# Moving tiles read alternately from their two halves, and products of 512 columns in place of 256 and 256

## The chip, the cores and the metric

The kernel runs on one core of a Trainium2 chip. Time is device time in microseconds; before the change the median of three runs is 1071.56 us (1071.44 to 1072.94). The engines meant below are TensorE (PE, with its weight loads, PEld), VectorE (DVE), ScalarE (ACT), GpSimd (POOL) and the DMA queues.

## What is computed

One layer of a hybrid decoder on 512 tokens of 1024 features, in float32: a gated feed-forward block, a mixer of two branches (spatial gating and a state-space scan), a second feed-forward block, gated embeddings and a last norm.

```python
def swiglu(x, w_gate, w_up, w_down):
    return (jax.nn.silu(x @ w_gate) * (x @ w_up)) @ w_down

h = h + 0.5 * swiglu(rmsnorm(h, ffn1_norm[i]), ffn1_w_gate[i], ffn1_w_up[i], ffn1_w_down[i])
proj = rmsnorm(h, mix_norm[i]) @ w_in[i]
u, v, z, xbc, dt_raw = jnp.split(proj, IN_SPLITS, axis=-1)
...
h = h + jnp.concatenate([ya, yb], axis=-1) @ w_out[i]
h = h + 0.5 * swiglu(rmsnorm(h, ffn2_norm[i]), ffn2_w_gate[i], ffn2_w_up[i], ffn2_w_down[i])
gate = jax.nn.sigmoid(rmsnorm(h, ple_norm[i]) @ ple_w_gate[i] + ple_b_gate[i])
h = h + gate * (p[i] @ ple_w_proj[i])
```

The feed-forward width is 2816, the input projection has 4624 columns (spatial gating 2 x 1024, z 1024, the convolved part 1536, 16 time steps).

## The kernel before

**Layout.** Features lie on the 128 partitions, tokens along the free dimension: the state `h` is eight tiles of 128 x 512. A matmul multiplies a stationary 128x128 piece of weights with a moving tile of tokens (up to 512 columns, one bank of PSUM) and adds into the bank. The moving tile is what the matmul streams column by column. Only the product for v is the other way round: there a chunk of 128 tokens is stationary and the weights move.

**Precision.** Every float32 operand of a large product is split into a rounded part hi and a rest lo (type float32r), and a product is three matmuls: hi x hi, hi x lo, lo x hi. The split of weights is `cast` on ScalarE (L532) and `low` on VectorE (L536), each 128x1024.

**Products, and the lines that issue them.**

- L746 (`Group.product`): gate and up products of ten of the eleven groups of the feed-forward block, done by a scheme of seven products of half size in place of eight. Each works on 256 tokens, so that a bank holds two results of 256 columns. Its inputs `xfa` and `xfb` (`XForms`, `Early`) hold pieces of 256 columns, hi beside lo.
- L835 (`plain_steps`): the first group of each block, without that scheme, for both halves of the tokens. The first input tile of a bank takes two matmuls over 512 columns and two over 256; the others take six over 256.
- L248 (`accumulate`): the down products (called with `halves`, eight output tiles, 22 input tiles), the output projection (all 512 columns, 16 input tiles) and the gates of the embedding (five with `halves`, three done one half after the other at the end of the kernel, `gate_half`).
- L232 (`passes`): the input projections, 28 units of 512 columns, and v, in widths of 272, 256 and 512.
- L1055 (`embedding`): the product of the per-layer embedding, two halves each.
- L338 (`spread`): a matmul with ones, which gives the norm's factor of each token to all partitions; its result is kept in a tile `r`, with which gate, up and projection results are multiplied.

**What reads the banks.** L951 adds a down product to `h`; `convin`, `z` and `u` are made from projections and `r` (L1225, L1478, L1621); L1679 adds the output projection; L1742 starts the gates at the end. L893 to L904 make the product of gate and up, `g`, and L915 and L917 split it into `ghi` and `glo`, the moving tiles of the down products.

**Order.** The work is a list of steps (`Step`: load, split, product, what comes after). `run` issues them in a fixed order, a hand-written string `ENTRY` moves pieces of them, and the order on TensorE, ScalarE, VectorE and the SP queue is the order of the program. Weights come in blocks of 512 KB over the SP queue, some with an adding DMA over the GpSimd queue. Of the eight banks three are called `mm`, two `a`, three `sm`.

Of the kernel before, what the change touches and what calls it, by code (L numbers as in the profile page):

```python
# [31 lines left out]
P = 128  # L32
# [80 lines left out]
def layer_kernel(ctx: ExitStack, tc: tile.TileContext, a: dict, out: bass.AP):  # L113
# [105 lines left out]
    def scaled_split(h, name, k):  # L219
# [18 lines left out]
    def accumulate(ps, w, j0, xs, first=True, last=True, parts=whole):  # L238

        whi, wlo = w  # L240
        for k, (xhi, xlo) in enumerate(xs):
            c = slice((j0 + k) * P, (j0 + k + 1) * P)
            by_part = [(n, tok) for tok in parts for n in range(3)]
            if k == 0 and parts is halves:
                by_part = [(0, whole[0]), (1, whole[0]), (2, halves[0]), (2, halves[1])]
            for i, (n, tok) in enumerate(by_part):
                wt, xt = ((whi, xhi), (whi, xlo), (wlo, xhi))[n]
                nc.tensor.matmul(  # L248
                    ps[:, tok], wt[:, c], xt[:, tok], start=first and k == i == 0,
                    stop=last and k == len(xs) - 1 and i == len(by_part) - 1, skip_group_check=True,  # L250
                )
# [22 lines left out]
    class Norm:  # L274
# [59 lines left out]
        @staticmethod  # L334
        def spread(diags, ps=None):
# [16 lines left out]
        def behind(self, steps, n, use):  # L352


            got = {}

            def sums():
                got["ps"] = self.sums()

            def spread():  # L360
                diags = self.diagonals(self.of_sums(got["ps"], n))
                got["ps"] = self.spread(diags, got["ps"])

            for step, fn in zip(steps, (sums, spread, lambda: use(self.kept(got["ps"])))):
                also(step, "after", fn)


    class RowNorm(Norm):
# [19 lines left out]
        def behind(self, steps, n, use):  # L388
            got = {}

            def factor():
                tok = self.of_sums(self.squares, n)
                yield
                got["diags"] = self.diagonals(tok)

            def spread():
                got["ps"] = self.spread(got["diags"])
# [213 lines left out]
    class Early:  # L611
# [58 lines left out]
        def form(both, i):  # L670
            n = (3, 2, 4).index(i) % 2
            for e in both:
# [12 lines left out]
                yield  # L685

    def by_half(t):
        return t.rearrange("p (m t) -> p m t", m=2)
# [28 lines left out]
    class Group:  # L717
# [17 lines left out]
        def product(self, i, to, fresh):  # L735
            whi, wlo = self.parts
            ps = self.ps[to]
            for p, xf in enumerate(self.xfs):
                xhi, xlo = xf.of(i)
                for m in range(2):  # L740
# [4 lines left out]
                    for n, (wt, xt) in enumerate(((whi, xhi), (whi, xlo), (wlo, xhi))):  # L745
                        nc.tensor.matmul(  # L746
                            o, wt[:, c], xt, start=fresh and p == m == n == 0,
                            stop=last and n == 2, skip_group_check=True,
                        )
# [62 lines left out]
        def plain_steps(self, first):  # L812


            def step(w, i, which, lower):
# [5 lines left out]
                def product():  # L821
# [5 lines left out]
                    for m, ps in enumerate(self.ps[which]):  # L827
                        for p, xf in enumerate(self.xfs):
                            c = slice((2 * p + m) * P, (2 * p + m + 1) * P)
                            t = (xf.a, xf.b)[lower]  # L830
                            by_part = [(n, slice(s, s + 1)) for s in range(2) for n in range(3)]
                            if p == 0:
                                by_part = [(n, slice(2)) for n in range(2)] + by_part[2::3]
                            for i, (n, s) in enumerate(by_part):
                                nc.tensor.matmul(  # L835
                                    by_half(ps)[:, s], (whi, whi, wlo)[n][:, c], t[:, s, n % 2],
                                    start=not lower and p == i == 0,
                                    stop=lower and p == len(self.xfs) - 1 and i == len(by_part) - 1,
                                    skip_group_check=True,
                                )  # L840
# [11 lines left out]
        def plain_gate(self):  # L852
            self.g = sb("g", (P, 2, 2, HT))
            for m, ps in enumerate(self.ps["gate"]):
                t = self.g[:, :, m]
                nc.vector.tensor_tensor(t, by_half(ps), by_half(self.shared["r"]), ALU.mult)
                yield
# [3 lines left out]
        def plain_finish(self):  # L861
            for m, ps in enumerate(self.ps["up"]):
                t = self.g[:, :, m]
                nc.vector.tensor_tensor(t, t, by_half(self.shared["r"]), ALU.mult)
                yield
                nc.vector.tensor_tensor(t, t, by_half(ps), ALU.mult)
                yield
# [15 lines left out]
        def gate_sum(self, half):  # L883
# [3 lines left out]
            ps, kept = ((self.ps["q"], self.u2), (self.ps["a"], self.p7))[half]  # L887
            nc.vector.tensor_tensor(self.g[:, half], by_half(ps), by_half(kept), ALU.add)

        def gate(self, half):  # L890

            t = self.g[:, half]
            nc.vector.scalar_tensor_tensor(t, t, -1.0, self.r(half), ALU.mult, ALU.mult)  # L893
# [3 lines left out]
        def times_r(self, half):  # L897
            t = self.g[:, half]
            nc.vector.tensor_tensor(t, t, self.r(half), ALU.mult)

        def finish(self, half):

            t = self.g[:, half]
            nc.vector.tensor_tensor(t, t, by_half(self.ps["xa"[half]]), ALU.mult)  # L904
# [18 lines left out]
    def swiglu(name, xfs, norm, closed, after, at):  # L923
# [8 lines left out]
        def down(part, gs_, i, n, last):  # L932
# [6 lines left out]
            def product(gs_=gs_, first=0, end=None):  # L939
                end = len(gs_) if end is None else end  # L940
                x = [t for g in gs_[first:end] for t in g.out]
                for k, d in enumerate(ds):
                    if first == 0:
                        ps[d] = sm_ps()
                    accumulate(
                        ps[d], (w.hi, w.lo), k * nf + 2 * first, x, first == 0, end == len(gs_), halves
                    )

            def add():
                for d in ds:  # L950
                    nc.vector.scalar_tensor_tensor(h[d], ps[d], 0.5, h[d], ALU.mult, ALU.add)  # L951
                    yield
# [59 lines left out]
    def embedding(q):  # L1012
# [34 lines left out]
        def product():  # L1047
# [3 lines left out]
            for k, n, i in sorted(order, key=lambda t: t[2]) if q else order:  # L1051
                (xhi, xlo), c = pe[k], slice((4 * k + i) * P, (4 * k + i + 1) * P)
                wt, xt = ((w.hi, xhi), (w.hi, xlo), (w.lo, xhi))[n]
                for tok in halves:
                    nc.tensor.matmul(  # L1055
                        ps[i][:, tok], wt[:, c], xt[:, tok], start=k == n == tok.start == 0,
                        stop=k == 1 and n == 2 and tok is halves[1], skip_group_check=True,
                    )

        def out():  # L1060
            for i, tag in enumerate(("embt", "embt", "p7", "u2", "rawd", "rawd", "rawd", "rawd")[4 * q : 4 * q + 4]):
                if tag in ("p7", "u2") or i % 2 == 0:
                    t = sb(tag, (P, 1 if tag in ("p7", "u2") else 2, T))
                    n = 0
                (nc.vector.tensor_copy if i > 1 else nc.scalar.copy)(t[:, n], ps[i])
                n += 1
# [152 lines left out]
    def conv(n, name, i, tag, to):  # L1219
        raws = {}  # L1220

        def begin():
            raw = raws["raw"] = sb("convin", (P, T + 3))
            nc.vector.memset(raw[:, 0:3], 0.0)
            nc.vector.tensor_tensor(raw[:, 3:], got[name]["ps"], mix["r"], ALU.mult)  # L1225
            o = raws["o"] = sb(tag)
# [247 lines left out]
    def gate_begins(j):  # L1474

        z = mix["z", j] = tmp()
        mix["th"] = tmp()
        nc.vector.scalar_tensor_tensor(z, got[f"z{j}"]["ps"], 0.5, mix["r"], ALU.mult, ALU.mult)  # L1478
        nc.scalar.activation(mix["th"], z, AF.Tanh)
# [139 lines left out]
    def u_kept(i):  # L1619
        t = sb("u")  # L1620
        nc.vector.tensor_tensor(t, got[f"u{i}"]["ps"], mix["r"], ALU.mult)  # L1621
        u.append(t)
# [45 lines left out]
    def out_step(d, which):  # L1668
# [9 lines left out]
        def add():  # L1678
            nc.vector.tensor_tensor(h[d], out_ps[d], h[d], ALU.add)  # L1679
            ffn2(d)  # L1680
# [58 lines left out]
    def gate(d, ps, tok, engine):  # L1739

        t = tmp()[:, tok]
        nc.vector.tensor_tensor(t, ps[:, tok], r[:, tok], ALU.mult)  # L1742
        nc.scalar.activation(t, t, AF.Sigmoid, bias=col("ple_b_gate", d))
# [85 lines left out]
def _laid_out(i):  # L1829
# [55 lines left out]
    wa[:, :, :, HT:DT_END] = w[:, 4608:].reshape(4, 2, P, HEADS).transpose(0, 2, 1, 3)  # L1885
    o["w_A"] = wa.reshape(4, P, 768)
    wb = np.zeros((9, P, HT), w.dtype)
    wb[:ND] = v[:, :, HT:T]
    o["w_W"] = np.ascontiguousarray(wb.reshape(3, 3, P, HT).transpose(0, 2, 1, 3).reshape(3, P, 3 * HT))
    o["w_v"] = np.ascontiguousarray(v[:, :, T:].reshape(4, 2, P, T).transpose(0, 2, 1, 3).reshape(4, P, 2 * T))  # L1890
    o["gm_w"] = np.ascontiguousarray(one["gm_w_s"].transpose(2, 0, 1).reshape(P, 8 * P))
# [31 lines left out]
```

## Time and profile before

| | |
|---|---|
| median of 3 runs | 1071.56 us (1071.44 to 1072.94) |
| span of the profiled execution | 1069.6 us; the page gives no other time for it |
| median less span | 2.0 us |
| matmuls | 7926, one weight load each |
| costliest lines on the chain | L248 34% (`sm` 25, `mm` 6, `a` 3), L746 35% (`mm` 20, `a` 15), L232 18%, L835 4% |
| DMA | 163.70 MB, 153 GB/s over the span; 343 GB/s in the first fortieth |

The page gives busy times of the engines, the span in forty slices and the chain of work that ended last. Matmuls overlap and their ends are modelled, so the busy time of a group is not its cost; how far apart the starts are is. The views used are the page, the chain of waits in order of time, the timeline, and busy time by stretch of the span.

### The profile page before, as it was taken

To read this page: it belongs to the slowest core of one execution; us is meant where nothing else is said; L and a number is where in the kernel's file an instruction comes from. 1 tells how busy PE (TensorE), PEld (TensorE's weight loads), DVE (VectorE), ACT (ScalarE), POOL (GpSimd) and SP (SyncE) were. 2 spreads that over 40 slices of the span, in tenths; PEclk is the share of its full clock that TensorE was granted. 3 is DMA by queue.
4 is the path that set the end of the run, shared out by engine and by line. 5 is a ranking of instruction groups with operands and counts; after the bars stand their busy time and mean duration, and the time that the engine had idled before them with its cause. 6 is when DMAs were issued, how large, how long until landed. Compare 5 with 4: busy or idle time off the path is not lost.

```text
span 1069.6 us, 19076 instructions
## 1 busy us (share of the span) xinstructions
PE 1059.4 (99%) x7926; PEld 993.5 (93%) x7926; DVE 781.0 (73%) x1082; ACT 513.8 (48%) x716; POOL 135.5 (13%) x125
## 2 busy tenths in 40 slices
PE   9999999999999999999999999999999999999997
PEld 8999999999999898887888888999999999999996
DVE  7987676766667686776998756687766677667766
ACT  7644444344444364664753434354444434443554
POOL 0100000000000300034333000001100000000311
PEclk9999999999999999999999999999999999999998
DMA  9987766666523232543431323667766676634412
GB/s 343 307 229 195 190 189 186 162 179 173 138 60 119 71 110 90 154 142 119 154 102 62 105 90 118 214 176 201 197 143 188 162 198 182 187 105 115 142 41 79
DMA packets 50327, 163.70 MB, mean 153 GB/s; under 512 B 5696, under 2 KB 6208, under 8 KB 50240
## 3 DMA queue, kind: packets, MB, share of 16 engines
q1 hardware_dynamic: 40304, 128.86, 35.0%
q0 software_dynamic: 8640, 31.46, 16.9%
q10 hardware_dynamic: 1296, 2.16, 0.7%
q8 instruction: 62, 1.02, 0.4%
q14 instruction: 25, 0.20, 0.1%
HBM read 158.20 MB, written 4.26 MB: 152 GB/s over the span
## 4 chain that ended last, share of the span: by engine, by line
PE 96%; DVE 1%; ACT 1%; DMA 1%; SPq 0%; issue 0%; DVEq 0%; ACTq 0%
PE sm L248 25%; PE mm L746 20%; PE a L746 15%; PE mm L232 7%; PE sm L232 7%; PE mm L248 6%; PE a L232 4%; PE a L248 3%; PE sm L835 2%; PE mm L835 1%; PE a L835 1%; PE sm L301 1%; PE sm L1388 1%; DMA g<-in_p 1%; PE sm L1632 1%; PE sm L1452 0%
## 5 line engine op out<-in xcount | busy, mean ns | idle before, releaser
L532 ACT CAST whi<-raw 128x1024 fp32r<-128x1024 f32 (+1 forms) x140 | 144.4, 1032 | 152.1 <-issue 56.2
L536 DVE TENSOR_TENSOR wlo<-raw,whi 128x1024 fp32r<-128x1024 f32 (+1 forms) x140 | 172.7, 1234 | 60.5 <-ACT whi L532 57.5
L746 PE MATMUL mm<-xfb,whi 128*128 128x256 f32 x960 | 166.1, 276 | 0.0
L248 PE MATMUL sm<-glo,whix 128*128 128x256 f32 (+1 forms) x512 | 151.1, 295 | 0.0
L248 PE MATMUL sm<-ghi,wlox 128*128 128x256 f32 x592 | 150.8, 277 | 0.0
L248 PE MATMUL sm<-ghi,whix 128*128 128x256 f32 (+1 forms) x512 | 150.4, 294 | 0.0
L746 PEld LDWEIGHTS mm<-xfb,whi 128*128 128x128 f32 x960 | 144.5, 188 | 0.0
L746 PE MATMUL mm<-xfb,wlo 128*128 128x256 f32 x480 | 132.5, 276 | 0.0
L248 PEld LDWEIGHTS sm<-ghi,wlox 128*128 128x128 f32 x592 | 111.2, 188 | 6.8
L746 PE MATMUL a<-xfb,whi 128*128 128x256 f32 x640 | 110.8, 276 | 0.0
L746 PEld LDWEIGHTS a<-xfb,whi 128*128 128x128 f32 x640 | 96.3, 188 | 0.0
L248 PEld LDWEIGHTS sm<-ghi,whix 128*128 128x128 f32 x512 | 96.1, 188 | 0.0
L248 PEld LDWEIGHTS sm<-glo,whix 128*128 128x128 f32 x512 | 96.1, 188 | 0.0
L746 PEld LDWEIGHTS mm<-xfb,wlo 128*128 128x128 f32 x480 | 90.1, 188 | 0.0
L536 DVE TENSOR_TENSOR wlox<-rawd,whix 128x1024 fp32r<-128x1024 f32 (+1 forms) x40 | 45.6, 1141 | 60.1 <-ACT whix L532 60.1
L746 PE MATMUL a<-xfb,wlo 128*128 128x256 f32 x320 | 88.3, 276 | 0.0
L536 DVE TENSOR_TENSOR wlo<-rawb,whi 128x1024 fp32r<-128x1024 f32 x52 | 63.6, 1222 | 18.6 <-ACT whi L532 18.5
L895 ACT ACTIVATE g<-g 128x512 f32<-128x512 f32 x40 | 25.3, 632 | 105.4 <-DVE g L893 105.4
L761 POOL DMA_DIRECT2D raw<-in_ffn_gu x20 | 17.3, 865 | 427.1 <-DVE h L951 164.7
L232 PE MATMUL sm<-x,whi 128*128 128x512 f32 x224 | 71.0, 398 | 0.0
L532 ACT CAST whi<-rawb 128x1024 fp32r<-128x1024 f32 x52 | 54.3, 1045 | 27.3 <-DVE rawb L756 17.6
L951 DVE SCALAR_TENSOR_TENSOR h<-sm,h 128x512 f32<-128x512 f32 x96 | 63.5, 683 | 4.4 <-PE sm L248 4.2
(388 smaller groups left out, 2498.0 us busy)
## 6 DMA issues: line engine op xcount, KB each, us to landing
raw<-in_ffn_gu SPq DMA_DIRECT2D x56, 512.0 KB, 6.6
rawd<-in_ffn_down SPq DMA_DIRECT2D x40, 512.0 KB, 4.6
rawb<-in_ffn_gu SPq DMA_DIRECT2D x32, 512.0 KB, 6.1
raw<-in_ffn_gu POOLq DMA_DIRECT2D x30, 512.0 KB, 5.5
raw<-in_w_in SPq DMA_DIRECT2D x28, 512.0 KB, 3.8
s<-in_ffn_gu SPq DMA_DIRECT2D x20, 512.0 KB, 7.7
s<-in_ffn_gu POOLq DMA_DIRECT2D x20, 512.0 KB, 8.9
raw<-in_w_out SPq DMA_DIRECT2D x16, 512.0 KB, 3.4
```

The source lines that it names most:

```text
L232: nc.tensor.matmul(ps, w, x, start=first and n == 0, stop=last and n == 2, skip_group_check=True)
L248: nc.tensor.matmul(ps[:, tok], wt[:, c], xt[:, tok], start=first and k == i == 0, stop=last and k == len(xs) - 1 and i == len(by_part) - 1 ...
L301: nc.tensor.matmul(ps[:, c : c + 1], part[:, c * P : (c + 1) * P], ones[:, 0:1], start=part is t, stop=part is not t or more is None,)
L532: nc.scalar.copy(self.hi[:, c], self.raw[:, c])
L536: nc.vector.tensor_tensor(self.lo[:, c], self.raw[:, c], self.hi[:, c].bitcast(F32), ALU.subtract)
L746: nc.tensor.matmul(o, wt[:, c], xt, start=fresh and p == m == n == 0, stop=last and n == 2, skip_group_check=True,)
L761: nc.gpsimd.dma_start(w21.raw, self.src[0], accum_op=ALU.add)
L835: nc.tensor.matmul(by_half(ps)[:, s], (whi, whi, wlo)[n][:, c], t[:, s, n % 2], start=not lower and p == i == 0, stop=lower and p == len(s ...
L895: nc.scalar.activation(t, t, AF.Silu)
L951: nc.vector.scalar_tensor_tensor(h[d], ps[d], 0.5, h[d], ALU.mult, ALU.add)
L1388: nc.tensor.matmul(ps, chunk(b_tok[g], c), to_state[g][c], start=True, stop=True)
L1632: nc.tensor.matmul(chunk(ps, c), chunk(v[c][i // 4], i % 4), chunk(ws[i // 4], i % 4), start=True, stop=True,)
```

## The change

A moving tile of 2n columns is no longer read as columns 0, 1, 2 ... but as 0, n, 1, n+1, 2 ...: the inner step of the read alternates between the two halves of the tile. The bank is still written in order, so a result comes out permuted. Where tokens move, the reader of the bank puts the order right with a read at a stride of two; r (from the factor spread) and the gate and up products are permuted alike, and the order is put right when `g` is split. Where weights move (v), the host lays their columns out permuted, and the result comes in order. The parts of `g` are stored in another order, so that a plain product's two halves lie side by side.

The down products, the plain gate and up products, the embedding and five of the gates go over 512 columns in one matmul, where they went over 256 and 256. L746 and the three gates by halves keep 256 columns, v its widths. All these walk in turns. The norm sums, the state-space scan, the spatial gating and the transposes are as before.

```diff
+    def turned(t, s=1):
+        return t.rearrange("p (s b i) -> p s i b", s=s, b=2) if s > 1 else t.rearrange("p (b i) -> p i b", b=2)
+
+    def back(ps):
+        return ps.rearrange("p (i b) -> p b i", b=2)
+
+    def two(t):
+        return t.rearrange("p (b i) -> p b i", b=2)
+
     def passes(ps, whi, wlo, xhi, xlo, first, last):
...
-                ps, w, x, start=first and n == 0, stop=last and n == 2, skip_group_check=True
+                ps, w, turned(x), start=first and n == 0, stop=last and n == 2, skip_group_check=True
...
             by_part = [(n, tok) for tok in parts for n in range(3)]
-            if k == 0 and parts is halves:
-                by_part = [(0, whole[0]), (1, whole[0]), (2, halves[0]), (2, halves[1])]
...
-                    ps[:, tok], wt[:, c], xt[:, tok], start=first and k == i == 0,
+                    ps[:, tok], wt[:, c], turned(xt[:, tok]), start=first and k == i == 0,
...
-                nc.tensor.matmul(ps, ones_r, diag, start=i == 0, stop=i == 1)
+                nc.tensor.matmul(ps, ones_r, by(diag), start=i == 0, stop=i == 1)
...
-                            o, wt[:, c], xt, start=fresh and p == m == n == 0,
+                            o, wt[:, c], turned(xt), start=fresh and p == m == n == 0,
...
-                            by_part = [(n, slice(s, s + 1)) for s in range(2) for n in range(3)]
-                            if p == 0:
-                                by_part = [(n, slice(2)) for n in range(2)] + by_part[2::3]
-                            for i, (n, s) in enumerate(by_part):
+                            for n in range(3):
                                 nc.tensor.matmul(
-                                    by_half(ps)[:, s], (whi, whi, wlo)[n][:, c], t[:, s, n % 2],
+                                    ps, (whi, whi, wlo)[n][:, c],
+                                    t[:, 0:2, n % 2].rearrange("p s (b i) -> p s i b", b=2),
...
-            g = self.g.rearrange("p h m t -> p m h t")[:, :, part]
-            hi, lo = (t[:, :, part] for t in (self.hi, self.lo))
+            g = self.g[:, :, part].rearrange("p m h (i b) -> p m h b i", b=2)
+            hi, lo = (t[:, :, part].rearrange("p m h (b i) -> p m h b i", b=2) for t in (self.hi, self.lo))
...
-                        ps[d], (w.hi, w.lo), k * nf + 2 * first, x, first == 0, end == len(gs_), halves
+                        ps[d], (w.hi, w.lo), k * nf + 2 * first, x, first == 0, end == len(gs_)
...
-                    nc.vector.scalar_tensor_tensor(h[d], ps[d], 0.5, h[d], ALU.mult, ALU.add)
+                    nc.vector.scalar_tensor_tensor(two(h[d]), back(ps[d]), 0.5, two(h[d]), ALU.mult, ALU.add)
...
-                for tok in halves:
-                    nc.tensor.matmul(
-                        ps[i][:, tok], wt[:, c], xt[:, tok], start=k == n == tok.start == 0,
-                        stop=k == 1 and n == 2 and tok is halves[1], skip_group_check=True,
-                    )
+                nc.tensor.matmul(
+                    ps[i], wt[:, c], turned(xt), start=k == n == 0,
+                    stop=k == 1 and n == 2, skip_group_check=True,
+                )
...
-        accumulate(ps, weights(a["ple_gate"][d], D), 0, x, parts=halves)
+        accumulate(ps, weights(a["ple_gate"][d], D), 0, x)
...
+    def in_turns(m):
+        return np.concatenate([m[..., ::2], m[..., 1::2]], axis=-1)
```

The other readers (`convin`, `z`, `u`, the output projection, the gates, the stored embedding) change as L951 does: `two(...)` around what lies in SBUF, `back(...)` around the bank. The weights of v go through `in_turns`.

More of the change, by code (lines that the diff above doesn't have):

```diff
@@ L685, in form, with by_col @@
                 yield
+    def by_col(t):
+        return t.rearrange("p h t -> p (h t)")
     def by_half(t):
@@ L830, in product @@
                             t = (xf.a, xf.b)[lower]
-                            by_part = [(n, slice(s, s + 1)) for s in range(2) for n in range(3)]
-                            if p == 0:
-                                by_part = [(n, slice(2)) for n in range(2)] + by_part[2::3]
-                            for i, (n, s) in enumerate(by_part):
+                            for n in range(3):
                                 nc.tensor.matmul(
-                                    by_half(ps)[:, s], (whi, whi, wlo)[n][:, c], t[:, s, n % 2],
-                                    start=not lower and p == i == 0,
-                                    stop=lower and p == len(self.xfs) - 1 and i == len(by_part) - 1,
+                                    ps, (whi, whi, wlo)[n][:, c],
+                                    t[:, 0:2, n % 2].rearrange("p s (b i) -> p s i b", b=2),
+                                    start=not lower and p == n == 0,
+                                    stop=lower and p == len(self.xfs) - 1 and n == 2,
                                     skip_group_check=True,
@@ L854, in plain_gate @@
             for m, ps in enumerate(self.ps["gate"]):
-                t = self.g[:, :, m]
-                nc.vector.tensor_tensor(t, by_half(ps), by_half(self.shared["r"]), ALU.mult)
+                t = by_col(self.g[:, m])
+                nc.vector.tensor_tensor(t, ps, self.shared["r"], ALU.mult)
                 yield
@@ L862, in plain_finish @@
             for m, ps in enumerate(self.ps["up"]):
-                t = self.g[:, :, m]
-                nc.vector.tensor_tensor(t, t, by_half(self.shared["r"]), ALU.mult)
+                t = by_col(self.g[:, m])
+                nc.vector.tensor_tensor(t, t, self.shared["r"], ALU.mult)
                 yield
-                nc.vector.tensor_tensor(t, t, by_half(ps), ALU.mult)
+                nc.vector.tensor_tensor(t, t, ps, ALU.mult)
                 yield
@@ L887, in gate_sum @@
             ps, kept = ((self.ps["q"], self.u2), (self.ps["a"], self.p7))[half]
-            nc.vector.tensor_tensor(self.g[:, half], by_half(ps), by_half(kept), ALU.add)
+            nc.vector.tensor_tensor(self.g[:, :, half], by_half(ps), by_half(kept), ALU.add)
         def gate(self, half):
-            t = self.g[:, half]
+            t = self.g[:, :, half]
             nc.vector.scalar_tensor_tensor(t, t, -1.0, self.r(half), ALU.mult, ALU.mult)
@@ L897, in times_r @@
         def times_r(self, half):
-            t = self.g[:, half]
+            t = self.g[:, :, half]
             nc.vector.tensor_tensor(t, t, self.r(half), ALU.mult)
         def finish(self, half):
-            t = self.g[:, half]
+            t = self.g[:, :, half]
             nc.vector.tensor_tensor(t, t, by_half(self.ps["xa"[half]]), ALU.mult)
@@ L1064, in out @@
                     n = 0
-                (nc.vector.tensor_copy if i > 1 else nc.scalar.copy)(t[:, n], ps[i])
+                (nc.vector.tensor_copy if i > 1 else nc.scalar.copy)(two(t[:, n]), back(ps[i]))
                 n += 1
@@ L1224, in begin @@
             nc.vector.memset(raw[:, 0:3], 0.0)
-            nc.vector.tensor_tensor(raw[:, 3:], got[name]["ps"], mix["r"], ALU.mult)
+            nc.vector.tensor_tensor(two(raw[:, 3:]), back(got[name]["ps"]), two(mix["r"]), ALU.mult)
             o = raws["o"] = sb(tag)
@@ L1477, in gate_begins @@
         mix["th"] = tmp()
-        nc.vector.scalar_tensor_tensor(z, got[f"z{j}"]["ps"], 0.5, mix["r"], ALU.mult, ALU.mult)
+        nc.vector.scalar_tensor_tensor(
+            two(z), back(got[f"z{j}"]["ps"]), 0.5, two(mix["r"]), ALU.mult, ALU.mult
+        )
         nc.scalar.activation(mix["th"], z, AF.Tanh)
@@ L1620, in u_kept @@
         t = sb("u")
-        nc.vector.tensor_tensor(t, got[f"u{i}"]["ps"], mix["r"], ALU.mult)
+        nc.vector.tensor_tensor(two(t), back(got[f"u{i}"]["ps"]), two(mix["r"]), ALU.mult)
         u.append(t)
@@ L1678, in add @@
         def add():
-            nc.vector.tensor_tensor(h[d], out_ps[d], h[d], ALU.add)
+            nc.vector.tensor_tensor(two(h[d]), back(out_ps[d]), two(h[d]), ALU.add)
             ffn2(d)
@@ L1741, in gate @@
         t = tmp()[:, tok]
-        nc.vector.tensor_tensor(t, ps[:, tok], r[:, tok], ALU.mult)
+        nc.vector.tensor_tensor(two(t), back(ps[:, tok]), two(r[:, tok]), ALU.mult)
         nc.scalar.activation(t, t, AF.Sigmoid, bias=col("ple_b_gate", d))
@@ L1885, in _laid_out @@
     wa[:, :, :, HT:DT_END] = w[:, 4608:].reshape(4, 2, P, HEADS).transpose(0, 2, 1, 3)
+    wa[..., :DT_END] = in_turns(wa[..., :DT_END])
     o["w_A"] = wa.reshape(4, P, 768)
     wb = np.zeros((9, P, HT), w.dtype)
[L1888 removed]
+    wb[:ND] = in_turns(v[:, :, HT:T])
     o["w_W"] = np.ascontiguousarray(wb.reshape(3, 3, P, HT).transpose(0, 2, 1, 3).reshape(3, P, 3 * HT))
[L1890 removed]
+    o["w_v"] = np.ascontiguousarray(in_turns(v[:, :, T:]).reshape(4, 2, P, T).transpose(0, 2, 1, 3).reshape(4, P, 2 * T))
     o["gm_w"] = np.ascontiguousarray(one["gm_w_s"].transpose(2, 0, 1).reshape(P, 8 * P))
```

6 lines of the change are left out of this document (3 added, 3 removed).

## The prediction

> **What bounds the kernel now.** I read the page first: busy times, slices, chain.
>
> ```profile
> span 1069.6 us, 19076 instructions
> ...
> PE 1059.4 (99%) x7926; PEld 993.5 (93%) x7926; DVE 781.0 (73%) x1082; ACT 513.8 (48%) x716; POOL 135.5 (13%) x125
> ...
> DVE  7987676766667686776998756687766677667766
> ...
> PEclk9999999999999999999999999999999999999998
> ...
> PE 96%; DVE 1%; ACT 1%; DMA 1%; SPq 0%; issue 0%; DVEq 0%; ACTq 0%
> ```
>
> TensorE is busy for 99% of the span at its full granted clock, and it is 96% of the chain that ended last. So the time of this kernel is a sum of matmul spacings, and anything that changes one spacing changes the end. A busy share does not tell how fast matmuls follow each other, because their modelled ends overlap. For that I took the chain in order of time, which gives start, length, and a count for stretches in which nothing but one line ran.
>
> ```profile
> 33.60 2.73 PE mm L835 x22
> ...
> 47.70 2.72 PE a L746 x24
> ...
> 605.57 5.44 PE a L248 x24
> ```
>
> L746 issues 256 columns each: 2.72/24 = 113.3 ns. In the third row L248 works for the output projection, 512 columns each: 5.44/24 = 226.7 ns, exactly twice. L835 mixes two of 512 with twenty of 256, in all 24 pieces of 256 columns: 2.73/24 = 113.8 ns. So a matmul here costs 0.443 ns per column and nothing per instruction; 256 and 256 cost what 512 cost. The limit is a rate. Which rate? The warm-up loop answers, in two rows of the timeline that start 1.28 us and three matmuls apart, and the granted clock of the last stretch stands beside it.
>
> ```profile
> 2.26 1.48 PE L197 MATMUL sm<-tmp 128*128 128x512 f32 x3
> ...
> 3.54 1.48 PE L197 MATMUL sm<-tmp 128*128 128x512 f32 x3
> ...
> 1063.00:1069.60 6.60, 0.00 (x0) 0.00 (x0) 2.06 (x6) 1.33 (x3) 0.00 (x0) 0.52 0.44 162
> ```
>
> 1.28/3 = 427 ns for 512 columns. The clock is recorded near one half only at the end of the span (0.52); I read the loop's 427 ns as the same half clock, for which the record at the start has no entry. At a full clock the array would then take 427/2 = 213.5 ns. The measured 226.7 is 1.062 times that, 17/16: one step is lost in every sixteen columns. The half-clock loop shows no such loss to speak of, so I take it for the supply of the moving tile, not for the array. The change alters precisely the order in which the moving tile is read.
>
> [...]
>
> **A second floor: the weight loads.** Each matmul loads its own 128x128 weights. Where the moving tile is short, only that load sets the spacing:
>
> ```profile
> 361.12 0.61 PE L301 MATMUL sm<-ones,ssum 128*128 128x1 f32 x5
> ...
> 361.12 0.95 PE L301 MATMUL sm<-ones,ssum 128*128 128x1 f32 x8
> ...
> 1056.58 0.60 PE L1809 MATMUL mm<-ident,h 128*128 128x128 f32 x4
> 1057.02 0.38 PE L1809 MATMUL a<-ident,h 128*128 128x128 f32 x2
> ```
>
> Three more one-column matmuls add 0.34 us, 113 ns each to the rounding; four transposes take 0.44 us, 110 ns each. Their weights are plain f32, not rounded, so they bound the rounded case and do not give it. A 256-column product at 113.3 ns therefore stands hardly above its weight load, one of 512 stands far above it. I use a floor of 111.5 ns.
>
> **The change part by part.** How many products are concerned comes from the loops and agrees with the counts by line (L746, L248, L835, L232, L1055):
>
> ```profile
> 0.00:1069.60 1069.60, 387.64 (x3360) 1.00 0.53 153
> ...
> 0.00:1069.60 1069.60, 379.94 (x2670) 1.00 0.53 153
> ...
> 0.00:1069.60 1069.60, 44.58 (x352) 1.00 0.53 153
> ...
> 0.00:1069.60 1069.60, 205.29 (x960) 1.00 0.53 153
> ...
> 0.00:1069.60 1069.60, 11.46 (x96) 1.00 0.53 153
> ```
>
> Products of 512 columns after the change: down products 2 x 8 x 22 x 3 = 1056, output projection 8 x 16 x 3 = 384, five whole gates of the embedding 5 x 8 x 3 = 120, plain gate and up products 192, embedding 48, input projections 28 x 8 x 3 = 672, the wide part of v 96, four factor spreads: 2572. Products that stay at 256 columns (or 272): L746 3360, the narrow parts of v 192, the three gates done by halves 144: 3696. The merging takes away 1174 matmuls and as many weight loads (856 down, 110 gates, 160 plain, 48 embedding).
>
> *The walk, 512 columns.* Bounds for the saving: nothing, if the lost step stays, and 226.7 - 213.5 = 13.2 ns, if it goes wholly; below nothing is the third rival. I take 11.2 ns (215.5 ns each), leaving 2 ns for the hand-over between matmuls, since the transposes, of 128 columns, do not go under 110 ns either. 2572 x 11.2 = 28.8 us.
>
> *The walk, 256 columns.* Bounds: nothing, and 6.6 ns, if the rounded loads were quicker than every load I can see. With the floor of 111.5 it is 1.8 ns. 3696 x 1.8 = 6.7 us. This is why most of the matmuls gain little: L746 keeps its pieces of 256.
>
> *The merging.* By today's rate it is worth nothing, 2 x 113.3 = 226.7. Under the new walk two pieces would cost 2 x 111.5 = 223 and one costs 215.5; this 7.5 x 1174 = 8.8 us is already in the 28.8. A bank is read only after its last product, so no reader loses an early half.
>
> *Reading back at stride two.* VectorE reads the banks of the down products (L951), the projections, the output projection and the gates in the order of tokens; the split of g (L915, L917) reads g at stride two instead of writing in another order. The instruction counts stay. No row shows a strided bank read. Bounds: nothing, and a doubling:
>
> ```profile
> L951 DVE SCALAR_TENSOR_TENSOR h<-sm,h 128x512 f32<-128x512 f32 x96 | 63.5, 683 | 4.4 <-PE sm L248 4.2
> ```
>
> A doubling would add 0.68 us to each of these 96. I take nothing, by the nearest row: it already reads one bank and one tile at a pace that its 512 elements set. For most stages even the doubling is covered, by VectorE's idle quarter; in two stretches it is not:
>
> ```profile
> 14.00:40.00 26.00, 26.00 (x213) 25.23 (x212) 25.62 (x47) 20.26 (x32) 1.90 (x2) 1.00 1.04 369
> ...
> 520.00:560.00 40.00, 40.00 (x249) 33.13 (x248) 39.59 (x72) 22.44 (x43) 14.34 (x10) 1.00 0.39 127
> ...
> 590.00:655.00 65.00, 65.00 (x296) 54.11 (x295) 38.71 (x60) 24.80 (x33) 1.30 (x1) 1.00 0.30 95
> ```
>
> Columns after the length are busy times of PE, PEld, DVE, ACT and POOL. Between 14 and 40 us VectorE is busy 25.62 of 26 and the DMA engines wholly (1.04, 369 GB/s); between 520 and 560 us VectorE 39.59 of 40. There TensorE cannot run ahead, and I take its gain back: about 5% of 40 us and 4% of 26 us, 3 us. The output projection (third row) has VectorE at 60%: the gain there should be whole.
>
> *The rest.* Permuted weight columns are laid out before the launch; the factor spreads and the order of g move with the products. No DMA, wait or queue is moved. Nothing.
>
> Sum: 28.8 + 6.7 - 3.0 = 32.5 us off the span, 1069.6 to 1037.1. The median lies 1071.56 - 1069.6 = 2.0 above the span: **1039 us**.
>
> **The rivals.**
>
> *No change.* The step lost in sixteen columns belongs to the rounded format or to the writing of the bank, which stays in order. Then all spacings stay, the merging gives nothing, and the time is 1071.6, within 2. For it: the ratio is the same for every tile and place. Against: the half-clock loop, same format, same bank, does not show it.
>
> *The walk is slower.* Every column now comes from another place than the one before. If each such change costs the step that today sixteen columns cost, a product takes 2 x 213.5 = 427 ns for 512 columns, and the 1003 us of concerned products (2572 x 226.7 + 3696 x 113.6) become 1003 x 32/17 = 1888: 1071.6 + 885 = 1957 us. It decides against the change from the point at which more than one column in sixteen loses a step. For it: reads in order are the ones whose price the trace shows, and it is hardly above the array's. Against: L746's inputs stand in tiles with other data between the pieces and pay nothing for that; but the trace has no column-by-column case. [...]
>
> *Only the reading back tells.* The walk changes nothing and the strided read doubles. VectorE has no room from 520 to 560 us, where 40/5.44, about seven, projections are read back: 7 x 0.68 = 4.8 us, and some 1.5 us from 14 to 40: 1078 us. From a price of about 0.2 us a read it would be seen.
>
> **How the numbers follow.** Walk supplies at or near the array's rate: 0.68, at 1013 (13.2 and 6.6 ns everywhere, 34.0 + 24.4 us) to 1060 (a third of the step regained). No change: 0.12. Walk slower: 0.14, far out. Reading back alone: 0.06. The range reaches to the third of these, 1012 to 1080, and leaves the slower walk out. The measurement tells 0.2% (2 us) from no change: faster 0.68, same 0.12, slower 0.20.
>
> **What would show it.** Right: in the chain, 24 of L248 in the output projection in about 5.17 us instead of 5.44, 24 of L746 in about 2.68 instead of 2.72, 7926 - 1174 = 6752 matmuls, L951 still near 683 ns, new idle time of PE near 15-40 and 520-560 us only. Wrong: 512 columns at 226.7 (first rival) or far above (second); 256 columns at 107 ns, the floor of the weight loads misjudged, worth up to 18 us more; L951 near 1300 ns.

## The result and the profile after

| | before | after |
|---|---|---|
| median of 4 runs | 1071.50 us (1071.41 to 1072.94) | 1040.27 us (1039.98 to 1040.75) |
| ratio after to before | | 0.9707, 95% interval 0.9693 to 0.9721 |
| span of the profiled execution | 1069.6 us | 1038.6 us |
| matmuls | 7926 | 6752 |

The kernel is 2.9% faster. The line numbers move: L746 is now L756, L248 is L255, L232 is L241, L835 is L842, L951 is L959. First the page of the changed kernel: span, busy times, VectorE by slices, the shares of the chain of work that ended last, and the line that reads back the down products.

```profile
span 1038.6 us, 16733 instructions
...
PE 1024.8 (99%) x6752; PEld 943.9 (91%) x6752; DVE 780.9 (75%) x1082; ACT 519.6 (50%) x716; POOL 135.6 (13%) x125
...
DVE  6987776777677787776998757698777767676776
...
PE 86%; DVE 8%; ACT 2%; issue 2%; DMA 1%; SPq 0%; POOL 0%; DVEq 0%; ACTq 0%; POOLq 0%
...
L959 DVE SCALAR_TENSOR_TENSOR h<-sm,h 128x512 f32<-128x512 f32 x96 | 62.2, 685 | 3.1 <-PE sm L255 3.1
```

TensorE is still the bound, but VectorE now holds 8% of the chain and ScalarE 2%, before 1% each: there are now places where TensorE waits for them. These shares are not the length of the waits. From a wait the chain is followed back along the engine that was waited for, for as long as that engine had work; the waits themselves come to a few microseconds (below).

Reading a bank at a stride of two costs VectorE nothing: 685 ns, before 683. Reading a tile in SBUF at a stride of two is not free. The split of `g`, which now reads `g` in this way, shows it (groups of instructions by line and shape, before and after):

```profile
L915 ACT CAST ghi<-g 128x1024 fp32r<-128x1024 f32 x20 | 21.1, 1053 | 45.8 <-DVE g L904 44.6 <-DVE g L866 1.2
...
L923 ACT CAST ghi<-g 128x1024 fp32r<-128x1024 f32 x20 | 27.3, 1364 | 46.1 <-DVE g L912 44.6 <-DVE g L874 1.5
```

ScalarE's part takes 1364 ns instead of 1053, VectorE's part (`glo`) 1372 instead of 1224. In the two runs below that read `g` in order (merge_only, gate_up_in_order) ScalarE's part is 1052 ns, in the two others that do not (walk_only, rest_later) 1375 and 1382. Why the bank's read stayed as it was is not separated: at 683 ns for 512 columns L951 took 1.33 ns a column already, and VectorE's part of the split goes from 1.20 to 1.34. Most of the extra time is hidden by idle time. VectorE's total hides it too (780.9 us, before 781.0), as other lines became shorter.

The chain in order of time shows the two prices of a product (start, length, count):

```profile
47.32 2.68 PE a L756 x24
...
92.52 5.18 PE sm L255 x24
...
602.68 5.18 PE mm L255 x24
```

2.68/24 = 111.7 ns for 256 columns (before 113.3), 5.18/24 = 215.8 ns for 512 (before 226.7, or twice 113.3), in the down products (second row) as in the output projection (third). The larger new waits stand in the timeline, each with its releaser in brackets:

```profile
27.39 0.59 PE L842 MATMUL sm<-xfb,whi 128*128 128x512 f32 x2
28.61 0.48 PE L842 MATMUL sm<-xfb,wlo 128*128 128x512 f32 x1 [0.63 <-DVE wlo L543]
...
322.33 0.38 PE L255 MATMUL sm<-ghi,wlo 128*128 128x512 f32 x1
322.92 0.48 PE L255 MATMUL sm<-ghi,whi 128*128 128x512 f32 x1 [0.20 <-ACT ghi L923]
323.69 0.48 PE L255 MATMUL sm<-glo,whi 128*128 128x512 f32 x1 [0.29 <-DVE glo L925]
324.01 0.38 PE L255 MATMUL sm<-ghi,wlo 128*128 128x512 f32 x1
...
729.82 0.38 PE L255 MATMUL sm<-glo,whix 128*128 128x512 f32 x1
730.65 0.48 PE L255 MATMUL sm<-ghi,wlox 128*128 128x512 f32 x1 [0.46 <-DVE wlox L543]
730.97 0.38 PE L255 MATMUL sm<-ghi,whix 128*128 128x512 f32 x1
...
984.66 0.38 PE L255 MATMUL mm<-x,wlo 128*128 128x512 f32 x1
985.64 0.94 PE L308 MATMUL sm<-ones,ssum 128*128 128x1 f32 x7 [0.61 <-POOL ssum L298]
```

The cost of a wait is the distance of the starts less the usual 0.216 us; the bracket is smaller, as it counts from a matmul's modelled end. Two matmuls start within the first row, the second 0.22 us later: 28.61 - 27.61 - 0.22 = 0.8 us. At 322 us three distances: 324.01 - 322.33 - 0.65 = 1.0 us; the same again at 960 us, in the other feed-forward block. At 729.8 us 1.15 - 0.43 = 0.7, at 984.7 us 0.8. Together 4.3 us. Smaller ones, of 0.5 us at 531 us and 0.2 us at 547 us, are not in this list.

The waits at 322 and 960 us are for the split of the last gate, one of those that became dearer. Its 512 columns take ScalarE 0.80 us there, before 0.62, and VectorE 0.74, before 0.69; so the strided read makes about 0.2 of the 1.0 us.

### The profile page after: what moved, and what is told of

Read it like the earlier page. It is cut to its first block, busy times and chain, and to the rows that moved or that the text cites. A ratio compares the mean times of both kernels' runs of the same rounds, so it can differ in the third digit from the quotient of the medians.

```text
span 1038.6 us, 16733 instructions
## 1 busy us (share of the span) xinstructions
PE 1024.8 (99%) x6752; PEld 943.9 (91%) x6752; DVE 780.9 (75%) x1082; ACT 519.6 (50%) x716; POOL 135.6 (13%) x125
## 4 chain that ended last, share of the span: by engine, by line
PE 86%; DVE 8%; ACT 2%; issue 2%; DMA 1%; SPq 0%; POOL 0%; DVEq 0%; ACTq 0%; POOLq 0%
PE sm L255 23%; PE mm L756 20%; PE a L756 15%; PE mm L241 6%; PE sm L241 5%; PE mm L255 4%; PE a L241 4%; PE a L255 3%; PE sm L842 1%; DVE wlo L543 1%; PE mm L842 1%; PE a L842 1%; DMA h<-in_x 1%; DVE tmp L1753 1%; PE sm L308 1%
## 5 line engine op out<-in xcount | busy, mean ns | idle before, releaser
L756 PE MATMUL mm<-xfb,whi 128*128 128x256 f32 x960 | 163.8, 275 | 0.0
L756 PEld LDWEIGHTS mm<-xfb,whi 128*128 128x128 f32 x960 | 147.1, 192 | 1.0
L756 PE MATMUL mm<-xfb,wlo 128*128 128x256 f32 x480 | 132.3, 276 | 0.0
L255 PE MATMUL sm<-ghi,wlox 128*128 128x512 f32 x296 | 112.4, 380 | 0.5 <-DVE wlox L543 0.5
L255 PE MATMUL sm<-ghi,whix 128*128 128x512 f32 x296 | 112.4, 380 | 0.0
L255 PE MATMUL sm<-glo,whix 128*128 128x512 f32 x296 | 112.3, 380 | 0.0
L756 PE MATMUL a<-xfb,whi 128*128 128x256 f32 x640 | 109.2, 275 | 0.0
L756 PEld LDWEIGHTS a<-xfb,whi 128*128 128x128 f32 x640 | 98.7, 192 | 1.1
L756 PEld LDWEIGHTS mm<-xfb,wlo 128*128 128x128 f32 x480 | 92.3, 192 | 0.0
L756 PE MATMUL a<-xfb,wlo 128*128 128x256 f32 x320 | 88.2, 275 | 0.0
L241 PE MATMUL sm<-x,whi 128*128 128x512 f32 x224 | 68.5, 388 | 0.0
L959 DVE SCALAR_TENSOR_TENSOR h<-sm,h 128x512 f32<-128x512 f32 x96 | 62.2, 685 | 3.1 <-PE sm L255 3.1
L255 PEld LDWEIGHTS sm<-ghi,wlox 128*128 128x128 f32 x296 | 56.1, 189 | 8.6 <-DVE wlox L543 0.9
L255 PEld LDWEIGHTS sm<-glo,whix 128*128 128x128 f32 x296 | 56.2, 190 | 6.8
L255 PEld LDWEIGHTS sm<-ghi,whix 128*128 128x128 f32 x296 | 56.2, 190 | 6.8
```

The source lines that it names most:

```text
L241: nc.tensor.matmul(ps, w, turned(x), start=first and n == 0, stop=last and n == 2, skip_group_check=True)
L255: nc.tensor.matmul(ps[:, tok], wt[:, c], turned(xt[:, tok]), start=first and k == i == 0, stop=last and k == len(xs) - 1 and i == len(by_p ...
L756: nc.tensor.matmul(o, wt[:, c], turned(xt), start=fresh and p == m == n == 0, stop=last and n == 2, skip_group_check=True,)
L959: nc.vector.scalar_tensor_tensor(two(h[d]), back(ps[d]), 0.5, two(h[d]), ALU.mult, ALU.add)
```

## The experiments

**One part of the change alone.** There are three such kernels. The first reads everything in order and keeps the merging:

```diff
     def turned(t, s=1):
-        return t.rearrange("p (s b i) -> p s i b", s=s, b=2) if s > 1 else t.rearrange("p (b i) -> p i b", b=2)
+        return t
```

(and in order, too: `back`, the plain products, the split of `g`, `in_turns`).

> All tiles read in order, banks read back in order, but 512 columns where the change has 512. Theory: spacings of 226.7 and 113.3 as before, time within 0.3% of before (1069 to 1075 us). Rival (merging, with 1174 weight loads fewer, is what gains): 1040 to 1050 us.

Measured: 1078.48 us (1078.31 to 1078.65), 1.0062 times before (1.0047 to 1.0077). It is neither of the two expected times: the merging alone costs 6.6 us. Its chain in order of time, a down product first, then the output projection:

```profile
109.12 5.59 PE sm L255 x24
...
614.86 5.44 PE mm L255 x24
```

The output projection is at 226.7 ns as before, but the down products take 5.59/24 = 232.9 ns for what before did in two pieces of 113.3. In-order reading has not one price but several; streams3 below shows something of what they depend on. The kernel before shows the dearer price as well, in the few down products that it sends over 512 columns (the first input tile of a call):

```profile
94.04 5.47 PE sm L248 x44
```

Four of these 44 matmuls have 512 columns, so all make 48 pieces of 256; at 113.3 ns they would take 5.44 us. In that trace the next start comes 236 ns after each of the 100 whole products that read `glo`.

The second keeps the walk and cuts the merged products in two, each half of the bank with its half of the walk:

```diff
+                for z in range(2 if cut else 1):
+                    o, m = ps[:, tok], turned(xt[:, tok])
+                    if cut:
+                        o, m = o[:, z * HT : (z + 1) * HT], m[:, z * P : (z + 1) * P]
```

> The alternating walk everywhere, but 256 and 256 columns where before had them (1174 matmuls and weight loads more than after). Theory (weight loads of 111.7 ns are the floor of a product of 256 columns): 1174 x (2 x 111.7 - 215.8) = 8.9 us above after, 1046 to 1051 us. Rival (the walk gains at any width, the merging nothing): 1040 us as after.

Measured: 1048.76 us (1048.62 to 1049.89), ratio to before 0.9787 (0.9773 to 0.9802), 8.5 us above after. So the walk alone is worth 1071.9 - 1048.8 = 23.1 us, the merging alone -6.6, and both together 31: the merging pays only with the walk. That 8.5 is so near the expected 8.9 is partly luck. The edit cuts more than the 1174 products that before had in two: it has 8168 matmuls against 6752, 1416 more, as it also cuts those that before sent whole. At 2 x 111.7 - 215.8 = 7.6 ns each that is 10.8 us; its slower products wait some 2 us less than those of after. Cut only where before cut, the walk alone would be worth a little more than 23.1 us. The down products of this kernel, in order of time, 48 pieces of 256 columns:

```profile
106.52 5.36 PE sm L259 x48
```

5.36/48 = 111.7 ns; before's pieces took 113.3 to 113.8, after's whole products 107.9 per 256 columns.

The third puts the gate and up products back in order, with their factor and the split of g:

```diff
-                            o, wt[:, c], turned(xt), start=fresh and p == m == n == 0,
+                            o, wt[:, c], xt, start=fresh and p == m == n == 0,
```

> As after, but the gate and up products read their tiles in order (3360 of 256 columns, 192 of 512), with their factor and the split of g in order too. Theory: 3360 x 1.7 + 192 x 10.9 = 7.8 us above after, about 1048 us. If products of 256 gained nothing from the walk: 2.1 us above after, 1042 us.

Measured: 1046.52 us (1045.88 to 1046.65), 6.3 us above after. A gate or up product in its chain:

```profile
112.79 2.73 PE mm L756 x24
```

That is 2.73/24 = 113.8 ns each; over all 3360 the starts lie 113.5 ns apart. The small gain at 256 columns is real. The run is 1.5 us below what was expected: the gate and up products take 9 us more than in after, those of 512 columns at 233 ns among them, but more than 2 us of the waits are gone, those at 322 and 960 us above all.

**The reading orders by themselves.** Three kernels (streams, streams2, streams3) issue sets of 36 matmuls, with one bank, no other engine at work and next to no DMA traffic during the sets; each set reads the moving tile in another order, and in some the weights lie elsewhere. From the chain, a set's length over 36 is the spacing.

> This kernel computes nothing of the reference: it sends 36 matmuls at a time past one another, each set with another reading order of the moving tile, one stationary tile, one bank, and no other engine or DMA at work. Theory (the lost step belongs to reading a tile of rounded floats in order, and goes when neighbouring columns come from two places): 512 columns in order 226.7 ns apart, alternating between halves 215.8; in turns of 16, 32, 64 or 128 columns 215.8 as well, if the two places only have to lie in different stretches of sixteen columns, and 226.7 for turns of 4 and 8, which stay within such a stretch; a tile of two-byte floats in order 215.8. 256 columns in order 113.3, alternating 111.7, which is the weight load: two columns alone 111.7 as well. Rival (the step was lost to other engines or DMAs at the same memory): 512 columns in order take 215.8 here too. Rival (it is the rounded format, not the order): the alternating ones take 226.7 here, and the gain in the kernel came from the merging.

```profile
15.23 8.16 PE ps_warm L39 x36
23.39 7.77 PE ps_warm L41 x36
31.16 7.77 PE ps_warm L43 x36
...
77.78 12.24 PE ps_warm L55 x36
...
183.00 7.79 PE ps_warm L75 x36
...
199.00 4.31 PE ps_warm L79 x36
203.31 4.02 PE ps_warm L81 x36
207.33 3.97 PE ps_warm L83 x36
```

L39 in order: 226.7 ns, with nothing else at work, so contention with other engines or DMAs falls. L41 halves in turns: 215.8, so the format as such falls too; L75 two-byte columns in order: 216. Two expectations missed: turns of four columns (0, 4, 1, 5, ..., L43) and of eight also take 215.8, although all their columns lie in one stretch of sixteen. Turns of 16 to 128 do so as expected. Not every alternation helps. Pairs from two places (0, 1, 256, 257, ..., L55) take 340 ns; runs of 4, 8 and 16 columns from two places 250, 243 and 240; single columns from four places in turn 283, from sixteen 435; all even columns before all odd ones 451.

At 256 columns in turns (L81) it is 111.7, and at 128 columns in order (L83) 3.97/36 = 110.3. Half the columns take nearly the same time, so at 256 the columns hardly set the spacing; that the weight load does is my reading, and in streams3 another reading of the weights beside the same moving tile changes it (120 ns, L96). At 256 columns in order (L79) it is 120, where 113.3 was expected and the kernel before shows 113.3; what makes the difference stays open.

The second set takes such orders at wider strides, shifts the two halves, reads two-byte columns at strides too, and ends with sets that shift the weights.

> As the first set of streams, nothing of the reference is computed. [...] Halves in turns 215.8 also when the tile begins at its third column or the halves are 258 apart. [...] Rival (any alternation between two places will do): turns of two columns, and halves in turns at a stride of two and four, all 215.8. [...]

```profile
31.21 8.19 PE ps_warm L44 x36
39.40 8.16 PE ps_warm L46 x36
47.56 16.31 PE ps_warm L48 x36
63.87 16.32 PE ps_warm L50 x36
80.19 16.61 PE ps_warm L52 x36
96.80 7.80 PE ps_warm L54 x36
104.60 7.80 PE ps_warm L56 x36
...
128.58 8.13 PE ps_warm L62 x36
136.71 16.26 PE ps_warm L64 x36
152.97 32.40 PE ps_warm L66 x36
185.37 17.44 PE ps_warm L68 x36
```

| reading order, 512 columns | measured, ns |
|---|---|
| in order | 227 |
| halves in turns; turns of four (streams) | 216 |
| turns of two (L44) | 228 |
| halves in turns, every second column (L46) | 227 |
| the same, every fourth (L48) | 453 |
| every second column in order (L50) | 453 |
| every fourth in order (L52) | 461 |
| two-byte: in order (streams, L75); every second, fourth, eighth (L62, L64, L66) | 216; 226, 452, 900 |

Halves in turns cost at a stride of two (L46) what reading in order costs at one, 227 ns, and at a stride of four (L48) what every second column in order costs, 453. Begun at the third column, or with halves 258 apart (L54, L56), they take 216.7, where 215.8 was expected. "Any two places will do" falls by L44 and L46.

No run shows what sets these times, and the table does not cover every order: pairs from two places take 340 ns, four places in turn 283, runs of 4, 8 and 16 from two places 250 to 240, and two-byte halves in turns (L68) 484. What a jump between places costs, and going back to a place, stays open. The granted clock (the figure after the brackets) fell during L66, in which a matmul came only every 900 ns:

```profile
153.00:160.00 7.00, 7.00 (x9) 0.86 (x8) 0.00 (x0) 0.00 (x0) 0.77 0.00 0
...
160.00:170.00 10.00, 10.00 (x13) 1.49 (x12) 0.00 (x0) 0.00 (x0) 0.50 0.00 0
170.00:185.00 15.00, 15.00 (x18) 2.04 (x17) 0.00 (x0) 0.00 (x0) 0.50 0.00 0
```

Yet the set kept its pace: 9 matmuls lie in the 7 us at 0.77, 13 and 18 in the 10 and 15 us at 0.50, those cut by an edge counted in, and all 36 take 32.40 us. So its spacing did not follow the granted clock. The sets that shift the weights came behind it, from 208 to 231 us, with the clock at 0.50, and tell nothing of the weights' places; streams3 asks that again.

Why, then, did merge_only's down products take 233 ns in order? The third set shifts the moving tile, or the weights in its place.

> As the other streams, nothing of the reference is computed. It asks why the in-order products of 512 columns took 233 ns in the down products of merge_only and 227 in the output projection. Theory (reading in order uses the supply to its last step, so it also pays when the moving tile and the weights lie unluckily to each other; in turns there is room to spare): in order 227 from column 0 and 230 to 236 from some other columns, and the same when the weights are shifted in place of the moving tile; in turns 215.8 to 218 from every column and with every place of the weights. Rival (the place of the moving tile alone decides): shifting the weights leaves 227. 256 columns in turns: 111.7 wherever weights begin, about 213 where every second column of weights is loaded, if the load is supplied as the moving tile is.

```profile
16.50 8.16 PE ps_warm L40 x36
24.66 8.41 PE ps_warm L42 x36
...
66.42 8.18 PE ps_warm L52 x36
...
90.53 7.77 PE ps_warm L58 x36
...
122.78 8.40 PE ps_warm L66 x36
...
147.94 8.17 PE ps_warm L72 x36
...
171.64 7.77 PE ps_warm L78 x36
...
208.07 4.02 PE ps_warm L94 x36
212.09 4.32 PE ps_warm L96 x36
```

In order from column 0 it takes 226.7 ns, from column 2 (L42) 234, from columns 4 to 32 between 229 and 233, from 64 (L52) and 128 again 227. Shifting the weights does much the same: by 2 to 32 columns 231 to 233 (by 8: L66), by 64 columns 227 (L72). In turns 215.8 from column 8 (L58) and with the weights 32 off (L78), and no more than 217 in any placing tried. So the place of the moving tile counts and that of the weights too, both are back at 227 at 64 columns off, and the reading in turns hardly feels it. The spacings are about those expected; that a supply is used to its last step, no run shows. Whether their distance decides or the place of each, these sets do not tell, as none shifts both. That the tiles of merge_only lie unluckily was not traced to their addresses. A product of 256 in turns takes 111.7 wherever the weights begin (L94), 120 where every second column of weights is loaded (L96), so the 213 expected there did not come.

**Moving a need behind a wait.** The waits at 322 and 960 us are for the split of the last gate.

```diff
-            if last and i == 0:
+            if last and i < 2:
...
+        p, q = pending[:2]
+        p.rest, q.product, q.rest = [q.product, p.rest], q.rest, None
         steps += pending
```

(one of the second step's two banks comes from `mm`.)

> As after, with the first part of the second of the last down products (12 matmuls, 2.6 us) sent ahead of the rest of the first one, in both blocks. Theory (the waits that came up behind the faster products are for the split of the last gate, which ends about 0.9 us too late): the waits of about 0.9 us at 322 and at 960 us go, 1038 to 1039 us. Rival (what follows waits by as much, as the order moves the need and not the split): 1040 us, as after.

Measured: 1038.78 us (1038.25 to 1040.27), ratio to before 0.9695 (0.9682 to 0.9708). In its timeline the first part of the second product (`whix`) follows without a gap where after had waited:

```profile
322.91 0.38 PE L255 MATMUL sm<-ghi,wlo 128*128 128x512 f32 x1
323.13 0.38 PE L255 MATMUL sm<-ghi,whix 128*128 128x512 f32 x1
```

Its span is 1037.1 us, 1.5 less than after; the two waits were worth 2.0. In this execution the first L756 started 0.4 us later than in after, behind longer waits for weights at 28 us; from there to the end it is 1.9 us shorter. The medians differ by 1.5 us, but the intervals of the ratios overlap, so the gap in the trace is the evidence, and the gain in time only agrees with it. Its median is the lowest measured.

## Why the prediction was right, and where it was not

The forecast was 1039 us, the measured time 1040.3.

- **A sum of spacings on TensorE:** right. By the two measured prices the products give 2572 x (226.7 - 215.8) = 28.0 and 3600 x (113.3 - 111.7) = 5.8 us, and the 96 of 272 columns 0.7 more; the span fell by 31.0. A term that the forecast did not have and one that it had too small pull against each other. By the starts in the traces, before paid 3.3 us more than these two prices, in products that were each some ns slower; and the waits among these products grew by 5.1 us, not 3. What is left of the balance, some 1.5 us, is the time of matmuls outside the sum. So it is partly luck that the sum came within 1.3 us; its main terms were measured one by one.
- **512 columns at 215.5:** 215.8. The bound, 213.5, was half of the warm-up's 427 ns, an estimate: no record shows that loop at half clock. The 216 of two-byte columns agrees with it; the 2 ns for the hand-over, for which no row of 512 columns stood, was a choice that held.
- **The cause, supply of the moving tile:** not shown. The supply and the step lost in sixteen columns were my reading of 226.7 against 213.5. What the runs show is that the reading order by itself moves the spacing of 512 columns: 226.7 ns in order, 215.8 in turns (streams, L39 and L41), 453 for every second column in order (streams2, L50). Turns of four and of eight columns, which stay within sixteen, take 215.8 too.
- **Floor of 111.5 for the weight loads:** 111.7 in turns, in every placing of the weights tried (streams3); 120 only where every second column of weights is loaded. walk_only shows what it costs not to merge: 8.5 us for 1416 products. The forecast's 8.8 was for 1174.
- **"By today's rate" the merging "is worth nothing":** wrong. Alone it costs 6.6 us, as in-order reading of the down products' tiles rises from 227 to 233 ns per 512 columns. I had read only the output projection's 226.7 and carried it over to other tiles. Before's own down products, done in pieces but for the first tile, showed the price only as 5.47 in place of 5.44 us, and I passed over it. It did no harm to the sum, since the walk removes that price too.
- **The strided read at nothing:** right for the banks, 685 against 683 ns; wrong for the split of `g`, which the forecast named beside them. There the read at a stride of two took ScalarE 1364 ns in place of 1053 and VectorE 1372 in place of 1224. The row that the forecast leaned on was of another operation, which took 1.33 ns a column from the start. The error cost little, as little of it reached TensorE.
- **3 us taken back between 14 and 40 and between 520 and 560 us:** half right. The first stretch gave back about what was said: the first product of L746 started at 39.4 us before and at 39.1 after (in rest_later at 39.5), a gain of 0.3 at most where the products ahead of it should have gained 1.6. For the second, four rows of the chains show the start of the same two products, before and after:

```profile
497.71 5.47 PE sm L232 x24
...
580.59 5.46 PE a L232 x24
...
482.62 5.18 PE sm L241 x24
...
563.28 5.18 PE a L241 x24
```

Between them lie 288 products of 512 columns, which should gain 288 x 10.9 = 3.1 us. They gained 82.88 - 80.66 = 2.2, so 0.9 us went back where 2 had been taken off. VectorE is busy for 49.52 of the 50 us from 500 to 550 us: here an engine that was nearly always busy was not late by all that the bound gained. The larger waits came up where a product's operand is finished just in time (322, 730, 960, 985 us); from 322 to 340 us VectorE has idle time (busy for 12.78 of the 18 us). The share of busy time could not show that; how long each operand was ready before its product would have.

- **The slower walk** fell: the walk takes 215.8 ns where it asked for 427. Orders that double the time exist: every second column in order costs 453 ns, halves in turns at a stride of four as well. That the walk escapes this because each of its halves is itself read in order is a guess; no run shows the reason.

## What to carry to other kernels

Before believing a matmul's price, divide spacing by columns in tiles of several places, and compare it with a stretch at a known lower clock: a spacing that stays as it is when the granted clock falls, as the 900 ns of L66 in streams2 at 0.77 and 0.50, is not set by that clock. For rounded float tiles, reading two in-order runs in turns cost less than one in-order run in every placing tried (215.8 to 217 ns for 512 columns against 226.7 to 236), and the permuted bank was read back for free (685 ns, before 683); the tile in SBUF that had to be read at a stride of two was not (1364 ns, before 1053), so look at every reader, and at lines rather than an engine's total. This bound got 2.9% faster and its larger new waits, 4.3 us together, came up at hand-overs with little slack, so list these, not the busiest stretches.

## What the runs showed of the hardware that was not expected

- Streaming 512 float32r columns in order takes 226.7 to 234 ns by where moving tile and weights lie (streams3), and 236 in some products of before; in turns 215.8 to 217 in all placings tried, and two-byte columns in order 216.
- Every second column of float32r in order takes 453 ns, twice the 226.7 of all in order; of two-byte columns every second takes 226, every fourth 452, every eighth 900. The set at 900 ns kept its spacing when the granted clock fell to 0.50.
- No product of 256 columns came under 111.7 ns (128 columns: 110.3), 4% more than half of the 215.8 of 512; that its weight load sets this is my reading.
- A read at a stride of two cost VectorE nothing from a bank (685 against 683 ns); for the same from SBUF ScalarE took 1364 ns in place of 1053 for 128 x 1024 float32.
